# A two-layer encoder trunk in fp32: the layer norms' shift row as a TensorE product, and own buffers for the modulation vectors' products

## The chip, the cores and the metric

The kernel runs on one core of one Trainium2 chip. The metric is the device time of one execution in microseconds (us). A core has five engines with an instruction queue each: PE (TensorE, matrix products; its weight loads are shown as PEld), DVE (VectorE), ACT (ScalarE), POOL (GpSimd) and SP (SyncE, which here only issues DMAs). An engine executes its own queue in order and waits on semaphores for the others.

## The reference

One sequence of 512 tokens with 1024 features goes through two layers, each a token mixer and an MLP. The modulation vectors come from a small conditioning vector c.

```python
for i in range(2):                       # layer 0: windowed attention, layer 1: RG-LRU block
    shift, scale, gate = split(silu(c) @ ada_w[i, 0] + ada_b[i, 0], 3)
    y = mixer[i](x * (1 + scale) + shift)
    x = layer_norm(ALPHA * x + (1 + gate) * y, ln_g[i, 0], ln_b[i, 0])
    shift, scale, gate = split(silu(c) @ ada_w[i, 1] + ada_b[i, 1], 3)
    y = square(relu((x * (1 + scale) + shift) @ mlp_w1[i])) @ mlp_w2[i]
    x = layer_norm(ALPHA * x + (1 + gate) * y, ln_g[i, 1], ln_b[i, 1])
```

There are four layer norms. The first three are followed by a modulated input of the next sublayer; called norm 0 (after attention), norm 1 (after the first MLP) and norm 2 (after the recurrent block) here. All matrices are float32 and are read once from DRAM.

## The kernel before, in words

**Products.** A float32 matrix product is done as three products in the fp32r format: each operand is split into a rounded part `hi` and a remainder `lo`, and hi*hi, hi*lo and lo*hi are summed in PSUM (`mm3`). Weights arrive by DMA in units of 128x1024 (512 KB) in one of four buffers `raw`. `conv_unit` splits a unit into one of six buffers `w`: ACT writes the rounded part (a CAST in the profile), DVE subtracts to get the remainder (a TENSOR_TENSOR `w<-raw,w`). The weight stream is strictly in order over the whole kernel.

**Order.** Python calls first only record operations (`Program.add`). A planner (`schedule`) then plays them through with estimated costs (`price`) and priorities (the place in the program plus an offset that the code shifts by the numbers in the table `P`) and so fixes the order of each engine's queue; `emit` (line 483) issues them. So nearly every instruction in the profile has line L483, and is told apart by its tiles. The DMA queue of SP has a fixed order too: a DMA that waits for its buffer holds all behind it.

**Stages.** Attention first (the QKV products, then eight heads one after the other, then the output projection), norm 0, the first MLP, norm 1, the recurrent block with norm 2, the second MLP and the last norm. The tokens are in four blocks `t` of 128. A sublayer's last products (`out_tiles`) come block by block, and `last_sink` follows each with `evac` (adds the residual, takes row statistics) and `ln_block`.

**A norm block** (`ln_block`, line 819). For each half `fh` of 512 features ACT normalizes in place, then DVE does two operations, `u = xh * rows[3]` and `h = u + rows[4]` (lines 859 and 860; `ex<-xb,rows` and `ex<-ex,rows` in the profile), where `rows[3]` and `rows[4]` hold gain and shift of norm and modulation together, copied to all 128 partitions. PE transposes `h` in four 128x128 pieces into one PSUM bank, and the split of that bank into `ht` (ACT and DVE) is the input of the next sublayer. A DMA from POOL that accumulates adds `ALPHA * ln_b` to the residual (line 881). The next sublayer's first products are done for token blocks 0 and 1 first and then 2 and 3 (`m_tiles` with `nsplit`).

**The combined rows** (`mod_rows`, line 787): three DVE operations over 128x1024 and two of ACT.

**Modulation vectors** (`gemv_tasks`, line 731). A vector of 1024 needs eight weight pieces of 128x1024; each is loaded into a `raw` buffer, and DVE multiplies it by a column of silu(c) and adds it to an accumulator (SCALAR_TENSOR_TENSOR `rows<-raw,sc,rows` or `acc<-raw,sc,acc`). At the end the 128 partitions are summed, by PE (attention) or POOL (first MLP). There are three vectors in attention and seven in the first MLP. They are cut into tasks that are called between the heads (`BH` tasks after each) or weight units. `keep_raw = 2` leaves two of the four `raw` buffers to them.

Of the kernel before, what the change touches and what calls it, by code (L numbers as in the profile page):

```python
# [70 lines left out]
def pack(inp):  # L71
# [91 lines left out]
    out["ident"] = np.eye(128, dtype=np.float32)  # L163
    return out
# [13 lines left out]
class View:  # L178
# [55 lines left out]
class Program:  # L234
# [60 lines left out]
    def price(self, op, reads, writes):  # L295
# [40 lines left out]
    def schedule(self):  # L336
# [36 lines left out]
        while len(order) < total:  # L373
# [101 lines left out]
    def emit(self, nc, tc, pools):  # L475
        fix = lambda a: self.real(a, pools)
        with tc.manual_schedule():
            order = self.schedule()
            self.place(order, pools)
            for op in order:  # L480
                args = [fix(a) for a in op.args]
                kw = {k: fix(a) for k, a in op.kw.items()}
                op.ins = getattr(getattr(nc, op.eng), op.fn)(*args, **kw)  # L483
# [3 lines left out]
        [128, "ht", "rows", "acc2"]  # L487
        + [f"ex{i}" for i in range(17) if i not in (12, 13)]
# [5 lines left out]
        + [f"hid{i}" for i in range(16)]  # L494
# [36 lines left out]
class Kernel:  # L531
    def __init__(self, I, O):
# [6 lines left out]
        self.ht = t("ht", 8192)  # L539
        self.hid = [t(f"hid{i}", 512) for i in range(16)]  # L540
        self.xb = [t(f"xb{i}", 1024) for i in range(TB)]
        self.rx = t("rows", 6144)
        self.rows = [self.rx[:, 1024 * i : 1024 * i + 1024] for i in range(5)]
        self.ex = [t(f"ex{i}", 512) if i not in (12, 13) else self.rx[:, 512 * i - 1024 : 512 * i - 512] for i in range(17)]
        self.ident = t("ident", 128)
# [12 lines left out]


    def renew(self, kind, idx):  # L560
        n = {"hid": 512, "xb": 1024, "ex": 512, "w": 2048}[kind]
        for i in idx:
            getattr(self, kind)[i] = self.region(f"{kind}{i}", n)
# [87 lines left out]
    def HT(self, k, lo=0, hi=512):  # L651
        a = k * 512
        return self.ht[:, a + lo : a + hi].bitcast(F32R), self.ht[:, 4096 + a + lo : 4096 + a + hi].bitcast(F32R)
# [5 lines left out]
    def fill(self):  # L659
# [16 lines left out]
        BH=3,  # L676
        QE='aavavavava',
        PE='ava',
        BO=(-100, 0, 100),
# [5 lines left out]
        AP0='vvvvvvvv',  # L685
# [16 lines left out]
        XV=(1, 1, 1),  # L702
    )
# [27 lines left out]
    def gemv_tasks(self, idx, part, acc, dst, sink_row=None, red=None, ap="vvvvvvvv"):  # L731
# [4 lines left out]
        def load(k):  # L736
            def f():
                if k < KT:
                    assert self.free_r
                    r = self.free_r.pop(0)  # L740
                    state[k] = r
                    nc.sync.dma_start(
                        out=self.raw[r][:, :], in_=self.I["adaw"][idx, k * 128 : (k + 1) * 128, part * D : (part + 1) * D]
                    )
# [3 lines left out]
                if k > 0:  # L748
                    r = state.pop(k - 1)
                    raw, c = self.raw[r][:, :], self.sc[:, k - 1 : k]  # L750
                    how = ap[k - 1]
                    if how != "v":
# [7 lines left out]
                    self.free_r.append(r)  # L760
# [26 lines left out]
    def mod_rows(self, shift, tmp):  # L787

        v = self.nc.vector
        r = self.rows  # L790
        v.scalar_tensor_tensor(out=tmp, in0=r[3][:, :], scalar=1.0, in1=r[2][:, :], op0=ALU.add, op1=ALU.mult)
        v.tensor_tensor(out=r[4][:, :], in0=shift, in1=tmp, op=ALU.add)
        v.scalar_tensor_tensor(out=r[3][:, :], in0=r[3][:, :], scalar=1.0, in1=r[1][:, :], op0=ALU.add, op1=ALU.mult)
        for i in (1, 2):
            self.nc.scalar.activation(out=r[i][:, :], in_=r[i][:, :], func=AF.Copy, scale=ALPHA)
# [23 lines left out]
    def ln_block(self, t, last=False, parts=1):  # L819
# [18 lines left out]
        for fh in range(2):  # L838
# [28 lines left out]
            hv = self.ht[:, a : a + 2048].rearrange("p (k n) -> p k n", k=4)[:, :, t * 128 : t * 128 + 128]  # L867
            lv = self.ht[:, 4096 + a : 4096 + a + 2048].rearrange("p (k n) -> p k n", k=4)[:, :, t * 128 : t * 128 + 128]
# [93 lines left out]
    def setup(self):  # L962
# [12 lines left out]
        self.mods = [Tile_("dr", f"mods{i}", 1024) for i in range(4)]  # L975
# [41 lines left out]
    def attn(self):  # L1017
# [7 lines left out]
        def OT(h, lo=0, hi=512):  # L1025
# [3 lines left out]
            a = (i - 4) * 1024  # L1029
            return self.ht[:, a + lo : a + hi].bitcast(F32R), self.ht[:, a + 512 + lo : a + 512 + hi].bitcast(F32R)  # L1030
# [88 lines left out]
        self.renew("ex", range(10))  # L1119
        self.keep_raw = 2  # L1120
# [29 lines left out]
        for n in range(2):  # L1150
# [6 lines left out]
            late.append((p, Q(6 + n, 0, 512)))  # L1157
        self.rope(late, self.P["QE"][8:])
# [85 lines left out]
        for h in order:  # L1244
# [7 lines left out]
        self.renew("ex", range(10))  # L1252
        self.renew("hid", range(8, 16))
        self.flush_bg()
        self.modes = self.P["OM"]
        self.mod_rows(accv, r[4])
# [45 lines left out]
    def load_mods(self, gate, shift, scale, ln, tmp):  # L1302
# [35 lines left out]
    def rnn(self, nsplit):  # L1338
# [6 lines left out]
        self.renew("ex", range(3, 9))  # L1345
        self.renew("hid", range(14, 16))
        xr = [self.hid[14][:, :], self.hid[15][:, :], ex[16][:, :]]
        XC = [ex[j] for j in range(3)]
        XCH = [ex[3 + j] for j in range(3)]
        XCL = [ex[6 + j] for j in range(3)]  # L1350
        GEL = [ex[9 + j] for j in range(3)]
# [126 lines left out]
        self.load_mods(0, 1, 2, 2, self.acc2)  # L1478
# [3 lines left out]
        self.renew("ex", range(3, 9))  # L1482
# [6 lines left out]
    def build(self, stop=99):  # L1489
# [3 lines left out]
        if stop == 1:  # L1493
            return self.dump()
        accs, red = (self.acc2, self.rows[1][:, :]), self.ex[8:10]
        gemvs = [(1, 2, self.rows[0], None), (2, 1, self.rows[3], None), (2, 0, self.rows[4], None)]
# [4 lines left out]
        self.bgq.append(lambda: self.mod_rows(self.rows[4][:, :], self.acc2))  # L1501
        self.bgq.append(self.rnn_cols)
        self.keep_raw, self.bg_rate = 2, self.P["RATE"]
# [12 lines left out]
        self.load_mods(3, None, None, 3, self.acc2)  # L1516
# [33 lines left out]
```

## Time and profile before

| | |
|---|---|
| median of 3 runs | 1193.3 us (1191.2 to 1193.58) |
| profiled execution | 1195.24 us |
| its span, first to last instruction | 1193.3 us |
| PE busy | 1137.3 us, 95% |
| DVE busy | 838.3 us, 70% |
| ACT busy | 523.7 us, 44% |
| mean granted clock of PE | 0.983 |
| weights read, 184 + 80 pieces of 512 KB seen in the records | 42% of the DMA engines' time on SP's queue |

The difference between the profiled execution and its span is time ahead of the first and behind the last instruction. Matmuls overlap, so PE's busy time counts a standing PE only where nothing is in flight; in a window of time the number of PE instructions shows a slow stretch as well. A window's row gives its length, then for PE, PEld, DVE, ACT and POOL the busy time and the number of instructions, the granted clock (1.00 is full), the DMA engines' share and GB/s. A timeline's row gives start, length, engine, line, operation, tiles and the number of merged instructions, and in brackets how long the engine stood idle ahead of it and what ended that.

### The profile page before, as it was taken

Reading aid. Unit: us, or ns where it says so; the run is one execution under the profiler, and the core shown is the slowest. Engines: PE = TensorE matmul, PEld = TensorE weight load, DVE = VectorE, ACT = ScalarE, POOL = GpSimd, SP = SyncE. Lnnn points to the kernel's source line nnn. Section 1 sums busy time; section 2 is a strip of 40 time slices with the busy share of each in tenths; the row PEclk is TensorE's granted clock in tenths of the full one; section 3 lists DMA queues with packets and bytes.
Section 4 is the critical chain, followed back from the end, with each engine's and each line's share of the span. In section 5 each row is a group of like instructions: output and inputs, shape, how many; then the busy total and the mean of one; then the engine's idle time right before and its main releaser. Section 6 shows DMA issues by size and latency. Waiting matters only on the chain.

```text
span 1193.3 us, 14277 instructions
## 1 busy us (share of the span) xinstructions
PE 1137.3 (95%) x5268; PEld 929.6 (78%) x5268; DVE 838.3 (70%) x1253; ACT 523.7 (44%) x774; POOL 95.7 (8%) x66
## 2 busy tenths in 40 slices
PE   6989998999999999999999998979999999999995
PEld 4877667988788878887887876868888888888885
DVE  8876979878878975449848888699744444444447
ACT  5455645512321342324368989824522322322411
POOL 1000000122222220000000000000100000000004
PEclk9999998999999999999999998989999999999998
DMA  9752663767677654222534574543732222222201
GB/s 348 287 188 76 212 246 106 196 210 247 200 246 244 247 195 154 100 95 55 151 106 121 139 181 111 151 142 125 211 106 89 99 95 91 104 88 106 89 1 71
DMA packets 56683, 179.99 MB, mean 151 GB/s; under 512 B 7891, under 2 KB 8403, under 8 KB 56614
## 3 DMA queue, kind: packets, MB, share of 16 engines
q1 hardware_dynamic: 53590, 170.44, 42.1%
q0 software_dynamic: 3024, 8.65, 4.0%
q8 instruction: 41, 0.67, 0.2%
q14 instruction: 28, 0.23, 0.1%
HBM read 160.56 MB, written 2.11 MB: 136 GB/s over the span
## 4 chain that ended last, share of the span: by engine, by line
PE 60%; DVE 16%; DMA 8%; ACT 8%; issue 4%; POOL 2%; SPq 1%; DVEq 0%; ACTq 0%; POOLq 0%
PE ps L483 60%; DVE ex L483 4%; DVE w L483 3%; DMA raw<-in_adaw 3%; DVE rows L483 3%; ACT w L483 2%; ACT rows L483 2%; POOL ex L483 2%; DVE xb L483 2%; DVE acc L483 2%; DMA rows<-w 1%; ACT L483 1%; DMA rows<-rows 1%; DVE st L483 1%; ACT ex L483 1%
## 5 line engine op out<-in xcount | busy, mean ns | idle before, releaser
L483 PE MATMUL ps<-ht,w 128*128 128x512 f32 (+1 forms) x2664 | 557.7, 370 | 3.1 <-ACT ht L483 1.8
L483 PEld LDWEIGHTS ps<-ht,w 128*128 128x128 f32 x2664 | 461.4, 190 | 90.1 <-ACT ht L483 2.7
L483 PE MATMUL ps<-w,hid 128*128 128x512 f32 (+1 forms) x1800 | 414.3, 390 | 2.2 <-ACT w L483 1.4
L483 DVE TENSOR_TENSOR w<-raw,w 128x1024 fp32r<-128x1024 f32 x192 | 237.2, 1240 | 226.7 <-ACT w L483 226.4
L483 PEld LDWEIGHTS ps<-w,hid 128*128 128x128 f32 x1800 | 334.1, 188 | 75.6 <-ACT w L483 1.8
L483 ACT CAST w<-raw 128x1024 fp32r<-128x1024 f32 x192 | 198.4, 1040 | 409.6 <-PE ps L483 304.8
L483 PE MATMUL ps<-w,ht 128*128 128x512 f32 (+1 forms) x336 | 75.5, 376 | 6.3 <-DVE w L483 5.2
L483 PEld LDWEIGHTS ps<-w,ht 128*128 128x128 f32 x336 | 57.5, 193 | 19.3 <-DVE w L483 5.6
L483 DVE SCALAR_TENSOR_TENSOR acc<-raw,sc,acc 128x1024 f32<-128x1024 f32 x40 | 55.4, 1385 | 17.1 <-DMA raw<-in_adaw 17.0
L483 DVE SCALAR_TENSOR_TENSOR ex<-rows,ps 128x512 f32<-128x512 f32 (+1 forms) x81 | 53.0, 671 | 19.7 <-PE ps L483 19.7
L483 DVE SCALAR_TENSOR_TENSOR rows<-raw,sc,rows 128x1024 f32<-128x1024 f32 x40 | 55.7, 1394 | 14.3 <-DMA raw<-in_adaw 14.1
L483 ACT ACTIVATE rows<-ps 128x512 f32<-128x512 f32 x66 | 39.1, 593 | 55.8 <-PE ps L483 55.7
L483 DVE TENSOR_TENSOR xb<-xb,ex 128x512 f32<-128x512 f32 (+1 forms) x81 | 55.8, 701 | 1.1 <-ACT xb L483 0.5
L483 DVE TENSOR_TENSOR hid<-ex,hid 128x512 fp32r<-128x512 f32 x66 | 45.5, 690 | 6.4 <-ACT hid L483 1.3
L483 DVE TENSOR_TENSOR ex<-rows 128x512 f32<-128x512 f32 x64 | 47.4, 742 | 1.6 <-ACT rows L483 1.5
L483 ACT ACTIVATE hid<-rows 128x512 fp32r<-128x512 f32 x64 | 40.5, 633 | 1.9
L483 ACT ACT_TABLE_LOAD x26 | 33.4, 1283 | 3.2 <-DMA w<-w 2.0
L483 PE MATMUL ps<-ident,ex 128*128 128x128 f32 x124 | 21.7, 294 | 13.6 <-DVE ex L483 13.5
L483 POOL TENSOR_TENSOR ex<-xb,rows 128x512 f32<-128x512 f32 x5 | 6.8, 1378 | 328.7 <-ACT xb L483 328.7
L483 POOL DMA_DIRECT2D xb<-rows x12 | 11.0, 919 | 262.3 <-DVE mv L483 136.3
L483 DVE TENSOR_TENSOR rows<-rows,ex 128x512 f32<-128x512 f32 x32 | 20.6, 683 | 15.4 <-DMA rows<-rows 12.4
L483 ACT ACTIVATE xb<-xb,mv 128x512 f32<-128x512 f32 x29 | 22.3, 810 | 19.9 <-DVE mv L483 19.8
(142 smaller groups left out, 803.8 us busy)
## 6 DMA issues: line engine op xcount, KB each, us to landing
raw<-in_W SPq DMA_DIRECT2D x184, 512.0 KB
raw<-in_adaw SPq DMA_DIRECT2D x80, 512.0 KB
ex<-in_ada0t SPq DMA_DIRECT2D x28, 256.0 KB
xb<-rows POOLq DMA_DIRECT2D x12, 512.0 KB, 5.9
rows<-w SPq DMA_DIRECT2D x16, 192.0 KB
raw<-in_W SPq DMA_DIRECT2D x8, 288.0 KB
rows<-rows SPq DMA_DIRECT2D x36, 64.0 KB
xb<-in_xT SPq DMA_DIRECT2D x8, 256.0 KB
```

Source lines behind the costliest of these rows:

```text
L483: op.ins = getattr(getattr(nc, op.eng), op.fn)(*args, **kw)
```

## The change

1. **Shift row.** The second DVE operation of a half block (line 860) goes; `h` is written by the multiplication alone. The shift is added after the transposes by one more fp32r product into the same bank: its weights `bm` hold the shift of that half as 4 rows of 128 features (rounded part in rows 0 to 3, remainder in rows 32 to 35), its moving operand `sel` is a 36x512 matrix of ones and zeros that spreads row j over columns 128j to 128j+127. The four transposes and the product are one accumulation group: only the first transpose opens the bank.
2. **Combined rows.** `mod_rows` keeps one of its three 1024-wide DVE operations. Shift and scale are written to DRAM as rows and read back as 4x256, with the norm's bias as `lnb4`, and combined there by DVE, ACT and POOL operations of 4x256 and less. The 512 KB broadcast of the shift ahead of norm 2 goes.
3. **Own buffers.** The modulation pieces no longer use `raw`: in attention they have two 128x1024 buffers of their own, and from the fourth head on six (four of them in the half of `ht` that is then free); in the first MLP three. `keep_raw` is 0. For this, several `ex` and `hid` buffers become halves of 1024-wide pairs, `ht` becomes two tiles, and the recurrent block's buffers are renumbered. The scratch of the recurrent block's column constants (`ex[10]`) thereby lies in one of the modulation buffers.
4. **Order.** Five tasks after each head, not three; their priority in attention is no longer raised by 100. Four of the eight pieces of the attention gate are multiplied by ACT and added by an accumulating DMA from POOL. The planner's costs for POOL's DMAs are refined.

```diff
         elif op.eng == "gpsimd" and op.fn == "dma_start":
-            op.cost = 1000
+            op.nbytes = w.shape[0] * n * 4
+            op.cost = 870 if "accum_op" in op.kw else 500
...
                 if op.fn == "dma_start":
-                    op.end += 4000
+                    if "accum_op" in op.kw:
+                        op.end += 5000 if op.nbytes > 300000 else 2600
+                    else:
+                        op.end += 2700 if op.nbytes > 100000 else 1500
...
+                if op.fn == "transpose" and kw:
+                    op.ins = nc.tensor.matmul(args[0], lhsT=args[1], rhs=args[2], is_transpose=True, stop=False, skip_group_check=True, **kw)
+                    continue
...
+        self.ex[0], self.ex[2] = self.pair("exa")
+        self.ex[4], self.ex[6] = self.pair("exb")
+        self.ex[10:12] = self.pair("exc")
+        self.big = [a[:, :].tile[:, :] for a in (self.ex[10], self.hid[10], self.ex[0], self.ex[4])]
...
-        BH=3,
+        BH=5,
-        BO=(-100, 0, 100),
+        BO=(0, 0, 100),
-        AP0='vvvvvvvv',
+        AP0='avavavav',
+        OWN=(0, 2, 3),
+        SW=3,
...
-                    assert self.free_r
-                    r = self.free_r.pop(0)
-                    state[k] = r
+                    state[k] = self.own[self.n_big % len(self.own)]
+                    self.n_big += 1
...
-                        nc.gpsimd.tensor_tensor(out=acc, in0=raw, in1=acc, op=ALU.add)
+                        nc.gpsimd.dma_start(out=acc, in_=raw, accum_op=ALU.add)
...
-    def mod_rows(self, shift, tmp):
+    def mod_rows(self, ln, shift, scale):
-        v.scalar_tensor_tensor(out=tmp, in0=r[3][:, :], scalar=1.0, in1=r[2][:, :], op0=ALU.add, op1=ALU.mult)
-        v.tensor_tensor(out=r[4][:, :], in0=shift, in1=tmp, op=ALU.add)
         v.scalar_tensor_tensor(out=r[3][:, :], in0=r[3][:, :], scalar=1.0, in1=r[1][:, :], op0=ALU.add, op1=ALU.mult)
...
+        self.renew("ex", (8, 9))
+        sel, tmp = r[4][0:36, 0:512], [self.acc2[0:4, i * 256 : i * 256 + 256] for i in range(3)]
+        nc.sync.dma_start(out=sel, in_=self.I["sel"])
+        nc.scalar.copy(out=self.ex[9][0:36, :].bitcast(F32R), in_=sel)
+        nc.sync.dma_start(out=tmp[0], in_=self.I["lnb4"][ln])
+        for i, row in ((1, scale), (2, shift)):
+            nc.sync.dma_start(out=tmp[i].rearrange("p (f c) -> p f c", f=2), in_=self.mods[row][0:1, :].quarters())
+        v.scalar_tensor_tensor(out=tmp[1], in0=tmp[1], scalar=1.0, in1=tmp[0], op0=ALU.add, op1=ALU.mult)
+        v.tensor_tensor(out=tmp[2], in0=tmp[2], in1=tmp[1], op=ALU.add)
+        nc.gpsimd.memset(self.ex[8][0:36, 0:256], 0.0)
+        nc.scalar.copy(out=self.ex[8][0:4, 0:256].bitcast(F32R), in_=tmp[2])
+        v.tensor_tensor(out=self.ex[8][32:36, 0:256].bitcast(F32R), in0=tmp[2], in1=self.ex[8][0:4, 0:256], op=ALU.subtract)
...
-                (v if self.par("GE") == "v" else nc.gpsimd).tensor_tensor(out=u, in0=xh, in1=self.rows[3][:, c], op=ALU.mult)
-                v.tensor_tensor(out=h, in0=u, in1=self.rows[4][:, c], op=ALU.add)
+                v.tensor_tensor(out=h, in0=xh, in1=self.rows[3][:, c], op=ALU.mult)
...
-                nc.tensor.transpose(pt[:, j * 128 : j * 128 + 128], h[:, j * 128 : j * 128 + 128], self.ident[:, :])
+                nc.tensor.transpose(pt[:, j * 128 : j * 128 + 128], h[:, j * 128 : j * 128 + 128], self.ident[:, :], start=j == 0)
+            bm, sel = self.ex[8][0:36, fh * 128 : fh * 128 + 128].bitcast(F32R), self.ex[9][0:36, :].bitcast(F32R)
+            nc.tensor.matmul(pt[:, :], lhsT=bm, rhs=sel, start=False, stop=True, skip_group_check=True)
...
-        self.keep_raw = 2
+        self.keep_raw = 0
+        self.own = self.big[:2]
...
+        self.renew_ht()
+        own = self.region("htl", 4096)
+        more = self.own + [own[:, i * 1024 : i * 1024 + 1024] for i in range(4)]
...
+            if i == self.P["SW"]:
+                self.own = more
             head(h)
             self.bg(self.P["BH"])
...
-        self.mod_rows(accv, r[4])
+        for row, src in ((4, r[3]), (5, accv)):
+            nc.sync.dma_start(out=self.mods[row][0:1, :], in_=src[0:1, :])
+        self.mod_rows(0, 5, 4)
...
-            nc.sync.dma_start(out=self.rows[4][:, :], in_=self.mods[shift][0:1, :].partition_broadcast(128))
-            self.mod_rows(self.rows[4][:, :], tmp)
+            self.mod_rows(ln, shift, scale)
...
-        self.keep_raw, self.bg_rate = 2, self.P["RATE"]
+        self.own = [self.big[i] for i in self.P["OWN"]]
+        self.bg_rate = self.P["RATE"]
```

More of the change, by code (lines that the diff above doesn't have):

```diff
@@ L163, in pack @@
     out["ident"] = np.eye(128, dtype=np.float32)
+    out["lnb4"] = np.ascontiguousarray(out["lnb"].reshape(4, 2, 4, 128).transpose(0, 2, 1, 3).reshape(4, 4, 256))
+    sel = np.zeros((36, 512), np.float32)
+    for j in range(4):
+        sel[[j, 32 + j], j * 128 : j * 128 + 128] = 1.0
+    out["sel"] = sel
     return out
@@ L482, in emit @@
                 kw = {k: fix(a) for k, a in op.kw.items()}
+                if op.fn == "transpose" and kw:
+                    op.ins = nc.tensor.matmul(args[0], lhsT=args[1], rhs=args[2], is_transpose=True, stop=False, skip_group_check=True, **kw)
+                    continue
                 op.ins = getattr(getattr(nc, op.eng), op.fn)(*args, **kw)
     LAYOUT = (
-        [128, "ht", "rows", "acc2"]
-        + [f"ex{i}" for i in range(17) if i not in (12, 13)]
+        [128, "hth", "htl", "rows", "acc2", "exa", "exb", "exc"]
+        + [f"ex{i}" for i in (1, 3, 5, 7, 8, 9, 14, 15, 16)]
         + [f"raw{i}" for i in range(4)]
@@ L493 @@
         + [192]
-        + [f"hid{i}" for i in range(16)]
+        + [f"hid{i}" for i in range(10)]
+        + ["hida"]
+        + [f"hid{i}" for i in range(12, 16)]
     )
@@ L538, in __init__ @@
         self.raw = [t(f"raw{i}", 1024) for i in range(self.NR)]
-        self.ht = t("ht", 8192)
+        self.ht = [t("hth", 4096), t("htl", 4096)]
         self.hid = [t(f"hid{i}", 512) for i in range(16)]
+        self.hid[10:12] = self.pair("hida")
         self.xb = [t(f"xb{i}", 1024) for i in range(TB)]
@@ L557, in region, with pair @@
         return Tile_("sb", name, n)
+    def pair(self, name):
+        t = self.region(name, 1024)
+        return [t[:, 0:512], t[:, 512:1024]]
     def renew(self, kind, idx):
@@ L562, in renew, with renew_ht @@
         for i in idx:
-            getattr(self, kind)[i] = self.region(f"{kind}{i}", n)
+            if kind == "hid" and i in (10, 11):
+                self.hid[10:12] = self.pair("hida")
+            else:
+                getattr(self, kind)[i] = self.region(f"{kind}{i}", n)
+    def renew_ht(self):
+        self.ht = [self.region("hth", 4096), self.region("htl", 4096)]
     def small(self, tag, n=4):
@@ L738, in f @@
                 if k < KT:
-                    assert self.free_r
-                    r = self.free_r.pop(0)
-                    state[k] = r
-                    nc.sync.dma_start(
-                        out=self.raw[r][:, :], in_=self.I["adaw"][idx, k * 128 : (k + 1) * 128, part * D : (part + 1) * D]
-                    )
+                    state[k] = self.own[self.n_big % len(self.own)]
+                    self.n_big += 1
+                    nc.sync.dma_start(out=state[k], in_=self.I["adaw"][idx, k * 128 : (k + 1) * 128, part * D : (part + 1) * D])
                 if k == 0:
@@ L748, in f @@
                 if k > 0:
[L749 to L750 removed]
+                    raw, c = state.pop(k - 1), self.sc[:, k - 1 : k]
                     how = ap[k - 1]
@@ L974, in setup @@
         self.st = {}
-        self.mods = [Tile_("dr", f"mods{i}", 1024) for i in range(4)]
+        self.mods = [Tile_("dr", f"mods{i}", 1024) for i in range(6)]
         cT, sg = self.small("cT", 8), self.small("sg", 8)
@@ L1243, in attn @@
         uo = N_WQ + 4
-        for h in order:
+        for i, h in enumerate(order):
+            if i == self.P["SW"]:
+                self.own = more
             head(h)
@@ L1300, in mlp, with load_mods @@
                 self.out_tiles(b + 12, 4, self.HID, lambda t, p: self.evac(t, 1, p, False), 0)
-    def load_mods(self, gate, shift, scale, ln, tmp):
+    def load_mods(self, gate, shift, scale, ln):
         nc = self.nc
@@ L1343, in rnn @@
         NW = self.NW
-        self.renew("ex", range(3, 9))
+        self.renew("ex", (1, 3, 5, 7, 8, 9))
         self.renew("hid", range(14, 16))
         xr = [self.hid[14][:, :], self.hid[15][:, :], ex[16][:, :]]
[L1348 to L1351, printed above, removed]
+        XC = [ex[j] for j in (0, 2, 4)]
+        XCH = [ex[j] for j in (1, 3, 5)]
+        XCL = [ex[j] for j in (7, 8, 9)]
+        GEL = [ex[j] for j in (6, 10, 11)]
         RI = {(i, j): self.rx[:, n * 512 : n * 512 + 512] for i in range(4) for j in range(3) for n in ((j * 3 + i) if i < 3 else 9 + j,)}
@@ L1500, in build @@
         self.bgq.append(lambda: self.load_ln_rows(1))
-        self.bgq.append(lambda: self.mod_rows(self.rows[4][:, :], self.acc2))
+        self.bgq.append(lambda: self.mod_rows(1, 5, 4))
         self.bgq.append(self.rnn_cols)
-        self.keep_raw, self.bg_rate = 2, self.P["RATE"]
+        self.own = [self.big[i] for i in self.P["OWN"]]
+        self.bg_rate = self.P["RATE"]
         self.ln_index = 1
```

34 lines of the change are left out of this document (19 added, 15 removed).

## The prediction

> **What bounds the kernel now.** I read the page's busy times first, then the windows by stage, then the waits, and the timeline of each place where TensorE (PE) stands still.
>
> ```profile
> PE 1137.3 (95%) x5268; PEld 929.6 (78%) x5268; DVE 838.3 (70%) x1253; ACT 523.7 (44%) x774; POOL 95.7 (8%) x66
> ...
> 59.50:189.00 129.50, 121.56 (x557) 90.42 (x555) 101.71 (x212) 72.59 (x159) 1.91 (x2) 0.99 0.52 175
> 189.00:198.00 9.00, 3.38 (x18) 2.55 (x17) 9.00 (x21) 5.05 (x8) 0.00 (x0) 0.81 0.35 117
> 198.00:558.70 360.70, 358.38 (x1681) 297.94 (x1680) 273.94 (x339) 117.29 (x151) 60.13 (x25) 1.00 0.56 183
> 558.70:577.00 18.30, 13.52 (x95) 12.28 (x94) 17.40 (x35) 8.02 (x13) 1.71 (x2) 0.91 0.46 109
> 577.00:842.00 265.00, 250.81 (x1163) 205.83 (x1162) 214.58 (x315) 188.53 (x277) 11.15 (x13) 0.97 0.47 137
> ...
> 860.00:1140.00 280.00, 280.00 (x1224) 229.68 (x1224) 126.93 (x154) 84.00 (x105) 0.00 (x0) 1.00 0.27 95
> ```
>
> The columns of a window are its length, then PE, PEld, DVE, ACT, POOL busy, the granted clock, DMA share and GB/s. From 860 to 1140 us, in the second MLP, PE is busy throughout: 280 us / 1224 = 0.229 us for a 128x512 product. Nothing but fewer products would help there, and the change takes none away. PE's idle time sits elsewhere: attention 129.5 - 121.56 = 7.9 us, layer norm 0 (after attention) 9.0 - 3.38 = 5.6, first MLP 2.3, layer norm 1 (after that MLP) 18.3 - 13.52 = 4.8, and 14.2 in the recurrent stage. In the two layer-norm windows VectorE (DVE) is busy for 9.00 of 9.00 and 17.40 of 18.30 us, so there DVE sets the pace. The waits say the same:
>
> ```profile
> PE ps L483 <- DVE ex L483: 13.5, 7, 4.3
> ...
> SPq L483 <- DVE w L483: 608.8, 163, 23.1
> ```
>
> A row is total us, times, longest. PE's largest wait is for `ex`, the normalized block that DVE hands to the transposes. The second row is the DMA queue waiting for a `raw` buffer to come free.
>
> **The change part by part.** First the shift row. Each half block loses one DVE addition, and each norm loses two 1024-wide DVE operations of `mod_rows`:
>
> ```profile
> L483 DVE TENSOR_TENSOR ex<-ex,rows 128x512 f32<-128x512 f32 x24 | 15.6, 682 | 0.0
> L483 DVE TENSOR_TENSOR rows<-rows,acc 128x1024 f32<-128x1024 f32 x2 | 2.4, 1216 | 0.0
> L483 DVE SCALAR_TENSOR_TENSOR mv<-mv 128x1 f32<-128x1 f32 x31 | 6.2, 240 | 0.1
> L483 PE MATMUL ps<-ex,w 96*128 96x512 f32 x108 | 26.4, 400 | 0.7 <-ACT rows L483 0.7
> ...
> 189.73 1.28 DVE L483 TENSOR_TENSOR ex<-ex,rows 128x512 f32<-128x512 f32 x2
> 190.46 1.26 PE L483 MATMUL ps<-ident,ex 128*128 128x128 f32 x8 [1.27 <-DVE ex L483]
> ...
> 195.34 1.28 DVE L483 TENSOR_TENSOR ex<-ex,rows 128x512 f32<-128x512 f32 x2
> 196.07 1.97 PE L483 MATMUL ps<-ident,ex 128*128 128x128 f32 x8 [4.35 <-DVE ex L483]
> ...
> 197.86 4.96 PE L483 MATMUL ps<-ht,w 128*128 128x256 f32 x26
> ```
>
> The 24 additions start about 0.6 us apart (a pair takes 1.28), so a norm loses 8 x 0.6 = 4.8 us of DVE, and `mod_rows` 2 x 1.2 = 2.4. It gains three DVE operations of 4x256: between 0.24 us (the 128x1 row) and 0.68 (the 128x512 row), taken in the middle at 0.4, because half the width is nearest to neither; 1.2 us together. PE gains 24 products of 36x512. A 96-row one costs 26.4 / 108 = 0.24 against 0.23 at 128 rows, so rows do not matter: 24 x 0.23 = 5.5 us, which costs nothing only where PE would stand idle.
>
> Layer norm 0: MLP products start at 197.86, after block 1, and DVE has had no idle time since 189. Ahead of that lie 4 additions and the two `mod_rows` operations, 2.4 + 2.4 - 1.2 = 3.6 us. The gate, scale and shift products also leave: four of DVE's steps now sit between 162 and 173 us, just ahead of the norm:
>
> ```profile
> 162.39 1.28 DVE L483 SCALAR_TENSOR_TENSOR rows<-raw,sc,rows 128x1024 f32<-128x1024 f32 x1
> ...
> 171.76 1.27 DVE L483 SCALAR_TENSOR_TENSOR rows<-raw,sc,rows 128x1024 f32<-128x1024 f32 x1
> ```
>
> With 5 tasks a head in place of 3 they come earlier. That is worth between 0 and 3.8 us more, since 5.6 us idle and 1.8 us of slow products (26 in 4.96 us is 0.19 each; at the 0.123 of the norm-2 row below they would take 3.2) bound the place at 7.4. I take 5.5, the middle. The trace shows the clock at 0.81 here. The Trainium skill ("TensorE: Matmul & The Clock Gate", "What's actually happening") says that PE falls to half rate after an idle window of about 3.4 us; with 4.35 us cut by 3.6 that window never fills, and by the rule alone the time would be some 1.8 us lower.
>
> Layer norms 1 and 2:
>
> ```profile
> 575.15 1.28 DVE L483 TENSOR_TENSOR ex<-ex,rows 128x512 f32<-128x512 f32 x2
> 575.88 0.66 PE L483 MATMUL ps<-ident,ex 128*128 128x128 f32 x4 [2.31 <-DVE ex L483]
> ...
> 833.58 5.67 PE L483 MATMUL ps<-ht,w 128*128 128x256 f32 x46
> ...
> 840.35 1.28 DVE L483 TENSOR_TENSOR ex<-ex,rows 128x512 f32<-128x512 f32 x2
> 841.09 1.32 PE L483 MATMUL ps<-ident,ex 128*128 128x128 f32 x8 [1.84 <-DVE ex L483]
> ...
> 842.42 12.81 PE L483 MATMUL ps<-ht,w 128*128 128x256 f32 x104
> ```
>
> In norm 1 the last block releases PE at 575.88; all 8 additions lie ahead of it in DVE's order, 4.8 us, less 0.3 for the product that the evacuation now waits for: 4.5 (ends 2.4, if only the 4 additions of blocks 2 and 3 count, and 4.8). In norm 2 PE's products end at 833.58 + 5.67 = 839.25 and go on at 842.42; of these 3.2 us, 0.9 are the transposes: 2.3 gained (ends 0.5, 2.3). There PE is the bound after that.
>
> End of the recurrent stage:
>
> ```profile
> 788.83 1.22 DVE L483 SCALAR_TENSOR_TENSOR acc<-rows 128x1024 f32<-128x1024 f32 x1
> ...
> 790.56 1.22 DVE L483 TENSOR_TENSOR rows<-rows,acc 128x1024 f32<-128x1024 f32 x1
> ...
> 792.84 1.22 DVE L483 TENSOR_TENSOR w<-raw,w 128x1024 fp32r<-128x1024 f32 x1
> ...
> 794.11 19.66 PE L483 MATMUL ps<-w,ht 128*128 128x512 f32 x74 [5.21 <-DVE w L483]
> ```
>
> PE waits 5.21 us for the weight remainder at 792.84, and two operations that go, 2 x 1.14 us by their spacing, stand ahead of it. The small ones that replace them may stand there too or later: 1.6 (ends 0, 2.3).
>
> Products with own buffers, first MLP: weights get all four `raw` buffers and the modulation three of their own.
>
> ```profile
> 325.96 0.74 PE L483 MATMUL ps<-w,hid 128*128 128x512 f32 x2 [1.37 <-ACT w L483]
> ...
> 442.41 7.83 PE L483 MATMUL ps<-w,hid 128*128 128x512 f32 x33 [0.86 <-DVE w L483]
> ```
>
> These two stalls are nearly all of its 2.3 us. The first waits for a cast of a weight, which an earlier load permits earlier; the second stands behind `mod_rows`. 1.9 gained (ends 0, 2.3).
>
> Attention: the same buffers, later priority for the tasks, and four of the gate's eight pieces go by ACT and an accumulating DMA from POOL.
>
> ```profile
> 78.69 4.53 PE L483 MATMUL ps<-hid,ex 128*128 128x256 f32 x10 [3.85 <-DMA ex<-rows]
> ...
> 151.66 1.28 DVE L483 SCALAR_TENSOR_TENSOR rows<-raw,sc,rows 128x1024 f32<-128x1024 f32 x1 [2.94 <-DMA raw<-in_adaw]
> ...
> 153.68 0.44 PE L483 MATMUL ps<-ident,ex 128*128 128x128 f32 x2 [1.86 <-DVE ex L483]
> ...
> DMA to landing us min/median/max: 4.4/5.9/8.4
> ```
>
> At 151.66 a modulation step waits 2.94 us for its load, softmax work is queued behind it on DVE, and PE loses 1.86. That goes. The 3.85 at 78.69 is the rotary embedding's DMA and mostly stays; a modulation step of 1.28 us ahead of it may move. I take 3.0 (ends -10 and 7.9): the last row is the landing of the existing accumulating DMAs; where one lands at the longest and not the median, 2.5 us later, DVE's next step waits with the softmax behind it, four times, 10 us. I take the gain, since the median is what the new cost table assumes (0.87 + 5.0). DVE loses 4 x 1.28 = 5.1 us, ACT gains about as much at 44% busy, POOL four issues at 8%.
>
> Moved and free: per norm SP issues four small DMAs more (selector, bias, two quarters; norms 0 and 1 also write shift and scale to DRAM), 0.33 us each by the second row below, and norm 2 one 512 KB broadcast less. Write, read, three DVE operations and a copy are about 2.2 + 2.2 + 2 = 6.4 us, by the 2.2 us of a small DMA here:
>
> ```profile
> 66.64 2.18 DMA ex<-rows
> ...
> 775.02 0.33 SPq L483 DMA_DIRECT2D rows<-mods  x1
> ...
> 176.38 0.59 ACT L483 COPY acc<-ps 128x512 f32<-128x512 f32 x1
> ...
> 218.65 0.26 DVE L483 TENSOR_SCALAR s<-ex 128x24 f32<-128x24 f32 x2
> ```
>
> In norm 0 the shift is ready at 177 (third row) and the first block at 190: hidden by the output projection's products; without that cover each us late costs one. The last row ends the recurrence's column constants, 33 tiny operations now at 214 to 219; their scratch becomes half of a modulation buffer, so they move behind the last product, near 435, under PE-bound work, and are due by 577. The new layout, the pairs and the single bank opening add no instruction.
>
> Sum: 3.0 + 5.5 + 1.9 + 4.5 + 1.6 + 2.3 = 18.8 us gained; of the 24 new products some 4 fall into idle time, 20 x 0.23 = 4.6 us paid: 14.2 us net. The profiled execution took 1195.24 (span 1193.3), so 1181.0; the median of the runs, 1193.3, is 1.9 lower: 1179.
>
> **The rivals.** *Larger gain*: norm 0 and attention give all they have (7.4 and 6), 4.9 more: 1174, and lower with the other ends; all ends together are 7.9 + 7.4 + 2.3 + 4.8 + 2.3 + 2.3 - 1.8 = 25.2, so 1168. For it: DVE's full windows. Against: DVE stays the one that is full there, 9.00 us in 9.00.
> *Small gain*: the stall passes to the row statistics, the ACT passes or the weight remainders that lie between, so that DVE's saving is only half PE's: 9.4 - 4.6 = 4.8 us, 1188.5. For it: between 190.46 and 196.07 DVE also did weight and `ht` remainders.
> *No change*: the shift row costs as much on PE as it frees and the buffers were not what was waited for: 1193.
> *Slower*: the accumulating DMAs in attention. Each delays a step on the in-order DVE, and the modulation load behind it holds SP, where weights queue. The attention gain of 3 is then lost, 11.2 us stay, and it decides from 11.2 / 4 = 2.8 us beyond the assumed 5.9, that is from 8.7 us of landing, against a longest of 8.4 now; at 11 us the four cost 20: 1193.3 - 11.2 + 20 = 1202. The Trainium skill ("SBUF — State Buffer", "SBUF: two separate sides") says that DVE operations of a two-port mode keep POOL from writing such a DMA's descriptors, which it measured as 3.1 us in place of 0.62; as an estimate from that page, 4 x 2.5 = 10 us, and the time would be 1192. The spread from 4.4 to 8.4 agrees with a delay of that size.
>
> **How the numbers follow.** Forecast, 1173 to 1187: 0.55. Larger gain, below 1173: 0.12. Small gain, 1187 to 1191: 0.13. No change within 0.2% (2.4 us, about what a measurement here can tell): 0.08. Slower: 0.12. Faster is 0.55 + 0.12 + 0.13 = 0.80. A range of 1168 to 1192 leaves out the slower case, a part of no change and the tail of the larger gain, about 0.2.
>
> **What would show it.** In the profile after: no `ex<-ex,rows` additions, 24 new products, DVE some 20 us less busy; in norm 0 the wait of 4.35 us below 1.5, the one at 575.88 about gone, none at 839; 794.11's wait near 3.5; the second MLP unchanged to 1 us. The forecast is wrong if PE's waits in attention grow (DVE behind a DMA into `rows`), if PE waits for the shift operand before a first block, or if the new plan opens waits where none are now.

## The result, and the profile after

| | before | after |
|---|---|---|
| median of the runs | 1193.4 us (1191.2 to 1194.9, 6 runs) | 1184.9 us (1184.8 to 1189.3, 6 runs) |
| profiled execution | 1195.24 us, span 1193.3 | 1187.53 us, span 1185.7 |

The ratio of the changed kernel to the one before is 0.994, with a 95% interval of 0.9921 to 0.9958; a second set of executions gave 0.9919 (0.9902 to 0.9935). So the change makes the kernel faster, by 8.5 us in the first set and 9.4 in the second. The direction was forecast, and 1184.9 lies in the range; but 14.2 us were forecast.

The page's busy times and the same windows as before:

```profile
PE 1146.8 (97%) x5292; PEld 932.8 (79%) x5292; DVE 822.9 (69%) x1228; ACT 530.3 (45%) x784; POOL 100.6 (8%) x73
...
59.50:189.00 129.50, 121.78 (x554) 90.43 (x553) 99.34 (x212) 77.50 (x166) 6.51 (x7) 0.97 0.61 194
189.00:198.00 9.00, 9.00 (x43) 7.00 (x42) 6.99 (x18) 6.61 (x9) 0.00 (x0) 0.90 0.59 167
198.00:558.70 360.70, 360.19 (x1687) 297.78 (x1687) 276.12 (x334) 119.99 (x156) 60.44 (x26) 1.00 0.52 179
558.70:577.00 18.30, 16.64 (x111) 14.50 (x110) 13.87 (x30) 6.92 (x11) 1.71 (x2) 0.91 0.63 161
577.00:842.00 265.00, 257.89 (x1218) 210.49 (x1217) 212.00 (x311) 193.39 (x284) 11.47 (x14) 0.99 0.49 139
860.00:1140.00 280.00, 280.00 (x1225) 229.66 (x1224) 125.14 (x151) 82.41 (x103) 0.00 (x0) 1.00 0.26 91
```

Two things are to be seen. First, the stalls went nearly as the prediction said: norm 0's window was 3.38 us busy of 9.00 and is now full, and PE's idle time from 577 to 842 fell from 14.2 us to 7.1. (The faster kernel does somewhat other work in a window of the same times; a comparison at equal work stands below.) Second, PE itself is busy 9.5 us longer (1137.3 to 1146.8), where 24 products at 0.23 us should have added 5.5. The idle time fell by 17.1 us (1193.3 - 1137.3 to 1185.7 - 1146.8); over half of that came back as busy time. The timeline of one block in the first MLP, where PE is the bound, shows how (PE first, then the weight loads):

```profile
545.45 0.60 PE L500 MATMUL ps<-ident,exa 128*128 128x128 f32 x4
545.98 0.49 PE L502 MATMUL ps<-ex,ex 36*128 36x512 f32 x1
546.40 0.66 PE L500 MATMUL ps<-ident,exa 128*128 128x128 f32 x4
546.99 0.50 PE L502 MATMUL ps<-ex,ex 36*128 36x512 f32 x1
547.41 1.88 PE L502 MATMUL ps<-w,hid 128*128 128x512 f32 x7
...
545.22 0.59 PEld L500 LDWEIGHTS ps<-ident,exa 128*128 128x128 f32 x4
545.98 0.18 PEld L502 LDWEIGHTS ps<-ex,ex 36*128 36x128 f32 x1 [0.17 <-issue]
546.39 0.42 PEld L500 LDWEIGHTS ps<-ident,exa 128*128 128x128 f32 x4 [0.24 <-DVE xb L502]
...
547.41 1.45 PEld L502 LDWEIGHTS ps<-w,hid 128*128 128x128 f32 x7 [0.25 <-issue]
```

Four transposes and the product take 0.95 us (545.45 to 546.40) and 1.01 (546.40 to 547.41). In the kernel before, eight transposes took 0.79, so four take 0.40, and the product costs about 0.58:

```profile
549.66 1.04 PE L483 MATMUL ps<-ident,ex 128*128 128x128 f32 x8
550.45 1.86 PE L483 MATMUL ps<-w,hid 128*128 128x512 f32 x7
```

The weight loads say why. A load usually starts while the product before it still runs (the transposes' first load at 545.22, they themselves at 545.45). That of the 36-row product starts with its product, 0.17 us after the last load ended, and the load behind it waits 0.24 us (the name DVE there is only the last semaphore: behind the second product the same 0.25 us stand with nothing waited for). So no weight load is taken ahead at either boundary; I read it as PE emptying before and after each of these products. The theory for the experiments is thus that the price of the product, 0.23 us, was the wrong term, and that its row count sets it. The rival is that adding onto a bank that transposes have just written is what costs. A second question was what had become of attention, which, counted up to the transposes at 194.46, seemed to take 134.9 us in place of 129.5.

### The profile page after: what moved, and what is told of

Its sections match the earlier page's. It is cut to its first block, busy times and chain, and to the rows that moved or that the text cites. A ratio compares the mean times of both kernels' runs of the same rounds, so it can differ in the third digit from the quotient of the medians.

```text
span 1185.7 us, 14389 instructions
## 1 busy us (share of the span) xinstructions
PE 1146.8 (97%) x5292; PEld 932.8 (79%) x5292; DVE 822.9 (69%) x1228; ACT 530.3 (45%) x784; POOL 100.6 (8%) x73
## 4 chain that ended last, share of the span: by engine, by line
PE 70%; DVE 11%; ACT 8%; DMA 7%; issue 3%; SPq 0%; DVEq 0%; ACTq 0%
PE ps L502 69%; DVE w L502 3%; ACT rows L502 3%; DVE rows L502 2%; ACT w L502 2%; ACT L502 1%; DMA rows<-rows 1%; DMA raw<-in_W 1%; DVE ex L502 1%; PE ps L500 1%; DVE acc L502 1%; DVE xb L502 1%; DMA rows<-w 1%; ACT ex L502 1%; ACT acc L502 1%
## 5 line engine op out<-in xcount | busy, mean ns | idle before, releaser
L502 PE MATMUL ps<-hth,w 128*128 128x512 f32 (+1 forms) x1776 | 505.4, 369 | 2.8 <-ACT hth L502 1.8
L502 PEld LDWEIGHTS ps<-hth,w 128*128 128x128 f32 x1776 | 321.8, 190 | 61.8 <-ACT hth L502 1.9
L502 PE MATMUL ps<-w,hid 128*128 128x512 f32 (+1 forms) x1581 | 368.9, 390 | 0.0
L502 PEld LDWEIGHTS ps<-w,hid 128*128 128x128 f32 x1581 | 295.1, 189 | 64.4 <-issue 0.7
L502 PE MATMUL ps<-htl,w 128*128 128x512 f32 (+1 forms) x888 | 326.8, 368 | 0.0
L502 PEld LDWEIGHTS ps<-htl,w 128*128 128x128 f32 x888 | 168.1, 189 | 29.4 <-issue 0.7
L502 PE MATMUL ps<-w,hth 128*128 128x512 f32 (+1 forms) x256 | 68.4, 373 | 2.8 <-DVE w L502 1.7
L502 DVE SCALAR_TENSOR_TENSOR ex<-rows,ps 128x512 f32<-128x512 f32 (+1 forms) x81 | 53.2, 674 | 13.8 <-PE ps L502 13.7
L502 PEld LDWEIGHTS ps<-w,hth 128*128 128x128 f32 x256 | 45.3, 188 | 13.0 <-DVE w L502 2.1
L502 PE MATMUL ps<-w,hida 128*128 128x512 f32 (+1 forms) x219 | 54.2, 388 | 0.0
L502 PEld LDWEIGHTS ps<-w,hida 128*128 128x128 f32 x219 | 40.9, 188 | 8.8
```

## The experiments

All ratios are to the kernel before, executed on the same chip in the same set; medians in us.

**128 rows.** Zero rows are added to both operands of the shift product:

```
-    sel = np.zeros((36, 512), np.float32)
+    sel = np.zeros((128, 512), np.float32)
...
-    nc.gpsimd.memset(self.ex[8][0:36, 0:256], 0.0)
+    nc.gpsimd.memset(self.ex[8][0:128, 0:256], 0.0)
```

> The shift row's product gets 128 rows in place of 36 (the added rows of both operands are zeros), nothing else changes. Theory A, the 36-row product is dear because its weight load isn't taken ahead of it: the 24 products go from a pace of 0.42 us or more to about 0.23, the weight loads' idle time of 4.0 us ahead of them goes, and of 24 x 0.2 to 0.3 us some 20 in 24 are on the path, so 4 to 6 us less than the changed kernel: 1179 to 1181 us, a ratio to before of 0.988 to 0.990. Rival B, it is dear because it adds onto a bank that the transposes have just written: rows change nothing, 1185 us, ratio 0.993, and the idle time of 4.0 us stays.

Measured: 1178.3 against 1196.4, ratio 0.9848 (0.9829 to 0.9867); theory A holds, with a gain larger than its 4 to 6 us. PE's busy time is 1133.0 us, 13.8 below the changed kernel's. The groups of PE and its weight loads, then one block of this kernel:

```profile
L502 PE MATMUL ps<-ex,ex 128*128 128x512 f32 x24 | 11.5, 478 | 0.0
L502 PEld LDWEIGHTS ps<-ex,ex 128*128 128x128 f32 x24 | 4.6, 190 | 0.0
...
540.04 0.60 PE L500 MATMUL ps<-ident,exa 128*128 128x128 f32 x4
540.40 0.48 PE L502 MATMUL ps<-ex,ex 128*128 128x512 f32 x1
540.71 0.60 PE L500 MATMUL ps<-ident,exa 128*128 128x128 f32 x4
541.07 0.48 PE L502 MATMUL ps<-ex,ex 128*128 128x512 f32 x1
541.39 0.85 PE L502 MATMUL ps<-w,hid 128*128 128x512 f32 x3
```

Three and a half times the rows, the same columns, and the unit takes 0.67 us where it took 0.95 and 1.01: 0.28 for the product. Note that the group's mean duration hardly differs (478 ns to 496); the starts tell, not the durations. The rival with the bank falls.

**64 rows and 68 rows**, by the same edit.

> The shift row's product gets 64 rows in place of 36 (zeros again). Theory, what counts is that the product leaves rows of the array unused in halves (up to 64 rows): as with 36, idle time of about 4 us ahead of the 24 weight loads, a pace of 0.42, the changed kernel's time within 2 us. Rival, the cost falls with every row added: about 0.33, and 3 us less than the changed kernel. Rival, what counts is that 36 isn't a multiple of 32: no idle time, and the time of the 128-row kernel, 0.985 of before.

> The same with 68 rows. Theory: just over half of the rows is as good as all of them: no idle time ahead of the weight loads, a pace of 0.23 to 0.25, and 6 to 8 us less than the changed kernel, ratio 0.985 to 0.988. Rival, the cost falls with every row: 0.33, 3 us less. Rival, multiples of 32: as the changed kernel.

Measured, beside the changed kernel once more in the same set:

> The changed kernel once more, beside the three below on one chip, so that small differences can be read. Expected: 7 to 9 us less than before (ratio 0.992 to 0.995); the granted clock between 84 and 100 us, 0.86 in the profile shown, near 1.00 if it was a matter of that one execution, and then the first MLP starts some 2 us earlier.

| kernel | median | ratio | 95% interval |
|---|---|---|---|
| changed kernel (36 rows) | 1186.1 | 0.9919 | 0.9902 to 0.9935 |
| 64 rows | 1187.5 | 0.9933 | 0.9916 to 0.9951 |
| 68 rows | 1179.1 | 0.9878 | 0.9858 to 0.9899 |
| before | 1195.5 | | |

The groups of the weight loads with 36 rows (changed kernel), 64 and 68; the last column is the idle time before them:

```profile
L502 PEld LDWEIGHTS ps<-ex,ex 36*128 36x128 f32 x24 | 4.4, 183 | 4.0 <-issue 4.0
```

```profile
L502 PEld LDWEIGHTS ps<-ex,ex 64*128 64x128 f32 x24 | 4.4, 183 | 4.0 <-issue 4.0
```

```profile
L502 PEld LDWEIGHTS ps<-ex,ex 68*128 68x128 f32 x24 | 4.8, 200 | 0.0
```

The starts say the same: four transposes and the product take 0.96 us with 64 rows (543.45 to 544.41) and 0.67 with 68 (536.54 to 537.21). 64 rows pay in full, 68 pay nothing: a step between the two, neither a slope nor a matter of multiples of 32. The Trainium skill ("TensorEngine Tiling (Array Packing)", "Key Properties") says that changing the tiling mode, not just the tile, drains the TensorE. The Trainium skill (the same page, "When to Use Tiling") gives row tiling for contract dimensions up to 64. The step between 64 and 68 and the 4.0 us of idle time agree with both; that a product of 36 or 64 rows switches this mode is my reading, no run shows the mode itself. The Trainium skill gives no price; here it is about 0.3 us for each change there and back. The clock between 84 and 100 us was 0.88 in this execution too, so that part of the expectation for the repeated kernel is wrong: it wasn't a matter of one execution.

**Two products in place of one.** Behind each shift product a second one with zero weights, onto the same bank, with 36 rows and with 128:

```
     nc.tensor.matmul(pt[:, :], lhsT=bm, rhs=sel, start=False, stop=False, ...)
+    nc.tensor.matmul(pt[:, :], lhsT=zero, rhs=sel, start=False, stop=True, ...)
```

> The changed kernel, and behind each 36-row product a second one of 36 rows whose weights are zeros, onto the same bank (24 more). If the price is paid where the row count changes (full array to half and back), the second product costs its columns alone, about 0.23 us: 24 x 0.23 = 5.5 us more than the changed kernel, 1190 to 1193, and idle time of about 4 us ahead of the weight loads as before. If each small product pays by itself, the second costs 0.4 to 0.6 as well: 10 to 14 us more, 1195 to 1200, and twice the idle time.

> The same with 128 rows in both: 24 more full products. Expected 24 x 0.23 = 5.5 us, less what falls beside waits, more than the 128-row kernel: 1182 to 1185, 0.988 to 0.991 of before. It gives what a full product costs on the path, and what the 36-row product's extra cost is to be compared with.

Measured against 1195.4: with 36 rows 1192.6, ratio 0.9971 (0.9956 to 0.9987), and with 128 rows 1186.1, ratio 0.9920 (0.9893 to 0.9948). One block with 36 rows twice, and its weight loads:

```profile
547.28 0.60 PE L500 MATMUL ps<-ident,exa 128*128 128x128 f32 x4
547.81 0.73 PE L502 MATMUL ps<-ex,ex 36*128 36x512 f32 x2
548.47 0.66 PE L500 MATMUL ps<-ident,exa 128*128 128x128 f32 x4
...
L502 PEld LDWEIGHTS ps<-ex,ex 36*128 36x128 f32 x48 | 7.3, 190 | 4.2 <-issue 4.2
```

The unit grew from 0.95 us to 1.19: the second small product costs 0.24, and the idle time stays at 4.2 though there are twice as many. So the price is that of the change of row count, not of a small product. The 128-row pair came out 1 us above its expectation; in its profile PE waits 2.89 us for a block of norm 0 where the single product's waits 0.42, and I didn't follow that further. The 36-row pair waits 2.0 us there, the changed kernel 0.3. So the pairs' whole times hold such a wait beside the products, and the price is better read from the block above.

**The parts alone.** The buffers without the shift product, and the shift product without the buffers:

```
# buffers alone: the changed kernel with
+    v.tensor_tensor(out=h, in0=u, in1=self.rows[4][:, c], op=ALU.add)
-    nc.tensor.matmul(pt[:, :], lhsT=bm, rhs=sel, ...)
-    self.mod_rows(0, 5, 4)
+    self.mod_rows(accv, r[4])
# shift product alone: the kernel before, with these lines the other way round
```

> The modulation's own buffers, its task rates and the accumulating DMAs in attention stay, the shift row is added by DVE again (old layer norm and old row preparation). Theory, attention's loss comes with the buffers and the norms' gain with the product: attention takes about 134 us, the norms stall as before, first MLP without its two stalls: 1193.4 + 5 - 2 = 1196, between 1193 and 1199. Rival, the buffers give what was forecast for them (3 in attention, part of norm 0, 1.9 in the first MLP): 1186 to 1189.

> The kernel before with the shift row's product and the new row preparation alone; old buffers, old task rates, gate vector by DVE. Theory, the norms gain by the product what the first expectation's products leave: norm 0 some 3.6, norm 1 4.5, recurrent stage 1.6 to 3.5, norm 2 2.3 to 5, together 12 to 16, less 20 x 0.45 = 9 for the products: 3 to 7 gained, 1186 to 1190, attention unchanged at 129.5. Rival, attention's loss comes with the shift row: attention takes 134 us here too, and the time is 1191 to 1195.

Measured: buffers alone 1199.1, ratio 1.0029 (1.0013 to 1.0046); shift product alone 1193.7, ratio 0.9982 (0.9969 to 0.9995). Alone, the buffers cost 2.7 us and the product gains 2.8; together they give 8 to 9. To see where, I compared executions at equal work: for the start of each PE instruction, how many columns had been streamed by then, the new products left out (2,408,452 in each kernel), and so the difference in time to the kernel before, taken at the ends of its stages. Minus is time gained in the stage, in us, each from one profiled execution:

| stage (us in the kernel before) | after | after, again | 68 rows | 128 rows | buffers alone | product alone |
|---|---|---|---|---|---|---|
| 0 to 60, set-up | +1.5 | +1.1 | +0.5 | +1.5 | +1.1 | +0.5 |
| 60 to 180, attention | -0.8 | -2.4 | -5.9 | -2.4 | -4.0 | +0.1 |
| 180 to 220, norm 0 | -0.9 | -2.1 | -3.7 | -4.7 | -8.2 | -3.5 |
| 220 to 540, first MLP | -2.8 | -2.9 | -2.8 | -2.9 | +9.8 | +1.6 |
| 540 to 600, norm 1 | -1.1 | +0.4 | -3.5 | -4.8 | +0.9 | +0.3 |
| 600 to 780, recurrent | -0.2 | +0.4 | +1.0 | +1.0 | +2.1 | +0.4 |
| 780 to 800, its end | -5.6 | -5.4 | -6.1 | -5.6 | +0.2 | -5.2 |
| 800 to 860, norm 2 | +1.7 | +1.7 | +0.3 | +0.3 | +4.9 | +1.7 |

(Attention differs by some us between executions: -5.9 is one in which PE's wait for the rotary embedding was 1.3 us and not 3.4 to 4.6. The executions shown for 68 rows, 1175.3 us, and for the buffers alone, 1202.1, lie 4 us below and 3 above their medians; the table shows where time goes rather than how much. Part of such differences is the clock, as the next section shows.) The theory that attention had lost by the buffers falls: it gained in each kernel with them. So the buffers alone came to the upper end of the forecast 1193 to 1199 by luck, and the product alone came into its rival's range without the rival's cause, since its attention is unchanged (+0.1). Attention's window looked longer because parts of the output projection, whose products run between norm 0's blocks, had moved. And buffers alone empty norm 0's stall by 8.2 us, more than with the product, and then lose 9.8 in the first MLP: PE waits there for weight remainders, between 200 and 400 us (total, times, longest):

```profile
PE ps L502 <- DVE w L502: 7.4, 3, 3.8
```

In the changed kernel the longest such wait there is 0.3 us.

**Norm 0 by DVE, norms 1 and 2 by a 128-row product**, to see whether norm 0 needs the product at all:

```
+    if self.ln_index == 0:
+        v.tensor_tensor(out=u, in0=xh, in1=self.rows[3][:, c], op=ALU.mult)
+        v.tensor_tensor(out=h, in0=u, in1=self.rows[4][:, c], op=ALU.add)
```

> The kernel with 128-row products, but layer norm 0 adds its shift row on DVE again; norms 1 and 2 by the product. Theory, norm 0's stall went with the modulation steps that were moved ahead of it and not with the shift row (buffers alone started the first MLP at 187.89 us, the 128-row product at 192.35): the first MLP starts 3 to 4 us earlier than with the product and the time is 1174 to 1176, 0.982 of before. Rival, the DVE time that comes back there is missed in the first MLP, as with the buffers alone, where PE waited 7.4 us more for weight remainders: the time is that of the 128-row kernel or up to 5 us more.

Measured: 1183.8, ratio 0.9902 (0.9889 to 0.9915). By the ratios that is some 6 us more than the 128-row kernel, and 4.8 more than the 68-row kernel of the same set; the rival holds, at the upper end of its 5 us or just past it. At equal work norm 0 gains 8.3 us, 3.6 more than in the 128-row kernel, but the first MLP loses 4.6 where that one gains 2.9. This wait of PE is there, with what DVE and POOL do at that time:

```profile
243.76 14.54 PE L502 MATMUL ps<-w,hid 128*128 128x512 f32 x56 [6.66 <-DVE w L502]
...
231.40 8.01 POOL L502 PARTITION_ALL_REDUCE rows<-acc  x2 [21.29 <-DVE acc L502]
...
234.06 2.18 DVE L502 SCALAR_TENSOR_TENSOR rows<-exc,sc,rows 128x1024 f32<-128x1024 f32 x1 [1.00 <-DMA exc<-in_adaw]
236.16 2.80 DVE L502 TENSOR_TENSOR hida<-ex,hida 128x512 fp32r<-128x512 f32 x1
...
241.29 1.27 DVE L502 SCALAR_TENSOR_TENSOR rows<-exa,sc,rows 128x1024 f32<-128x1024 f32 x1
242.49 1.21 DVE L502 TENSOR_TENSOR w<-raw,w 128x1024 fp32r<-128x1024 f32 x1
```

So DVE time that norm 0's additions take, 4.8 us, is missed 50 us later, in the first MLP's weight remainders. That it is missed there is shown by these two kernels: the sum over partitions behind the same modulation steps starts at 231.40 here and at 227.75 in the 128-row kernel, 3.7 us later. The wait has other parts too: beside that sum two operations take 2.18 and 2.80 us in place of 1.28 and 0.68, and DVE waits 1.00 us for a load; the 128-row kernel has such slow operations as well, earlier, and PE does not wait for them. How I read it is that own buffers let the modulation steps come in a denser row on DVE, and that only the shift row's DVE time makes room for them, so that the parts don't add up. That reading is not shown: each kernel is planned anew, and another order of the queues may account for a part.

**The gate's pieces by DVE again** (`AP0='vvvvvvvv'`), to price the accumulating DMAs:

> In attention all eight pieces of the gate vector are added by DVE again, as before the change (no ACT scaling, no accumulating DMAs from POOL there); the rest is the changed kernel. Theory, the accumulating DMAs delay the rotary embedding's small DMAs and DVE's steps: the wait of 3.57 us ahead of 82.93 goes, attention takes 130 us or less from 59.5 in place of 134.9, and the time is 4 to 5 us less, 1180 to 1181. Rival, attention lost by something else of the change (more loads in flight, five tasks a head in place of three, the order of the rotary embedding): attention stays at 134 or more, and the time at 1185, or 1186 to 1189 where DVE's 4 x 1.28 us more count.

Measured: 1185.6, ratio 0.9911 (0.9889 to 0.9933), not to be told from the changed kernel's 0.9919. The windows from 72 to 84 and 84 to 100 us, of the changed kernel and of this one:

```profile
72.00:84.00 12.00, 7.68 (x30) 5.27 (x29) 6.95 (x16) 7.49 (x16) 0.87 (x1) 0.90 0.91 274
84.00:100.00 16.00, 15.76 (x62) 11.20 (x60) 11.12 (x36) 10.28 (x28) 0.85 (x1) 0.86 0.42 111
```

```profile
72.00:84.00 12.00, 10.71 (x42) 7.42 (x41) 11.24 (x25) 5.98 (x16) 0.00 (x0) 1.00 0.85 289
84.00:100.00 16.00, 11.96 (x48) 6.73 (x47) 14.62 (x31) 10.05 (x25) 0.00 (x0) 1.00 0.68 219
```

PE's wait for the rotary embedding does go from the first window, and comes back in the second in small waits behind a DVE that is busy 14.62 of 16 us. The theory was wrong that anything is gained by it. (The execution shown is the fastest of the six, 1180.1 us, with a mean granted clock of 0.995 where the changed kernel's has 0.988; the others took 1182.6 to 1189.1.)

The 128-row kernel is faster than this one and than the changed kernel; it can't be told from the one with 68 rows.

## Why the prediction was right and wrong

*The price of the 24 products (wrong, and the main miss).* The step was "A 96-row one costs 26.4 / 108 = 0.24 against 0.23 at 128 rows, so rows do not matter". The row came from the wrong side of a step: 96 rows are on the full array's side, 36 are not. 24 products at 0.58 us are 13.9 us in place of 5.5. On the chip the difference between 36 rows and full rows is 8.7 us (18.1 gained by 128 rows, 9.4 by the changed kernel in its second set) or 7.0 (16.4 by 68 rows, in the same set); the starts in the blocks give 24 x 0.30 = 7.2 of it. With full rows, at nearly the price forecast, the change gives 16 to 18 us, near the 14.2. That this is so near is in part luck: the end of the recurrent stage gave 4 us more than its term, norm 2 and attention less than theirs.

*End of the recurrent stage (size).* 1.6 forecast, 5.6 and 5.4 measured in the changed kernel, 5.2 with the product alone, nothing with the buffers alone. The wait at 794.11 was to be near 3.5 and is 1.71. The rest, about 2 us, is the clock. Windows of the kernel before and of the changed one, and the products behind the wait in each:

```profile
780.00:800.00 20.00, 14.53 (x52) 10.98 (x52) 17.34 (x22) 6.50 (x7) 0.00 (x0) 0.83 0.44 148
...
794.11 2.50 PE L483 MATMUL ps<-w,ht 128*128 128x512 f32 x5 [5.21 <-DVE w L483]
```

```profile
777.00:792.00 15.00, 12.97 (x55) 9.88 (x54) 14.90 (x20) 7.64 (x9) 0.00 (x0) 1.00 0.43 146
...
786.31 0.50 PE L502 MATMUL ps<-w,hth 128*128 128x512 f32 x1 [1.71 <-DVE w L502]
```

Before, 5.21 us of idle time were followed by ten products that start 0.43 us apart, half the pace of the 0.23 behind them; after 1.71 us there is no slow stretch. The prediction reckoned with the clock in norm 0 and forgot it here.

*Norm 0 (right on the stall, wrong on what follows).* 5.5 us were forecast, 0.9 and 2.1 measured, 4.7 with 128 rows. The wait of 4.35 us was to fall below 1.5. It is gone, products of the output projection now stand in its place; the one wait of size left, 1.17 us, is that ahead of the first block, 1.27 before. But eight products at 0.58 us are paid here, and in this execution the clock still fell:

```profile
185.00 0.63 PE L500 MATMUL ps<-ident,exa 128*128 128x128 f32 x4 [1.17 <-DVE exa L502]
...
184.30:187.70 3.40, 2.70 (x13) 1.78 (x14) 3.11 (x5) 1.90 (x4) 0.30 (x1) 0.96 0.00 0
187.70:191.20 3.50, 3.50 (x10) 2.77 (x9) 2.96 (x9) 0.72 (x1) 0.55 (x1) 0.55 0.76 150
...
187.68 3.69 PE L502 MATMUL ps<-w,hid 128*128 128x512 f32 x9
```

In the first stretch PE runs eight transposes, two shift products and three others beside the end of the wait, in the second it is full and has 0.55 of its clock, some 1.6 us lost. In the second execution the clock stays at 1.00 from 180 to 196. So the step "that window never fills" failed in one execution of two. The Trainium skill ("TensorE: Matmul & The Clock Gate", "Part 4: PE-mode transpose") adds that transposes don't count as PE-busy in the same way; these two rows agree with that. The Trainium skill (the same page, "What's actually happening") says that the window of about 3.4 us runs freely; that fits the two executions. In all traces here, after the first 20 us and ahead of the last 20, the clock stands at half for 3.4 or 6.8 us at a time.

*Norm 1 (wrong).* 4.5 us gained, less the products, was forecast; 1.1 us gained and 0.4 lost came, and 4.8 gained with 128 rows. The wait at 575.88 was to be about gone. With 36 rows (first two lines) and with 128 (last two) it is:

```profile
571.15 0.63 PE L500 MATMUL ps<-ident,exb 128*128 128x128 f32 x4 [1.66 <-DVE exb L502]
573.10:576.00 2.90, 2.90 (x11) 2.57 (x11) 1.16 (x2) 0.59 (x1) 0.86 (x1) 0.50 0.45 89
...
564.05 0.63 PE L500 MATMUL ps<-ident,exb 128*128 128x128 f32 x4 [1.87 <-DVE exb L502]
560.00:580.00 20.00, 18.13 (x127) 16.49 (x126) 16.21 (x30) 8.90 (x14) 1.71 (x2) 1.00 0.56 143
```

So full rows don't shorten the wait, and that their 4.8 us lie near the forecast is luck. What differs is the products' price, 8 x 0.30 = 2.4 us, and the clock behind the wait, 0.50 with 36 rows (in both executions) and 1.00 with 128. One execution with 128 rows doesn't show that full rows keep the clock up: with 68 rows it was at half for 3.4 us near this norm.

*First MLP (right).* 1.9 forecast, 2.8 and 2.9 measured: of both stalls 0.3 us is left, and the second MLP is unchanged at 280.00. *Norm 2 (right on the wait, the products mis-priced).* None is left at 839, but the products cost more than that gives: 2.3 less 1.8 was forecast, 1.7 were lost, with full rows 0.3.

*Attention (right in sign, not in its reasons).* 3.0 forecast, 0.8 and 2.4 measured, and 1.1 to 1.5 us lost in the set-up, which the prediction did not look at. The accumulating DMAs land in about the time assumed, 5.9 us (the last number is the median to landing; the four take 4.4 to 5.9):

```profile
rows<-exc POOLq DMA_DIRECT2D x4, 512.0 KB, 5.1
```

The slower rival needed 8.7, and the delay of POOL's descriptors that the prediction estimated from the Trainium skill doesn't show. But the 5.1 us that DVE saves there are worth nothing that can be measured: the kernel that gives them back takes the same time.

*The rival "small gain"* (1187 to 1191) came near the total but not the cause: the stalls did not pass to DVE's other work, TensorE's own time grew. *DVE some 20 us less busy* was 15.4. *The column constants* are 24 tiny operations of DVE, not 33; they moved to 405 to 418 us and no wait of PE stands there.

## What to carry to other kernels

A product with 36 or 64 rows among full ones was not a small product but two changes of row count: padding with zeros to 68 or 128 rows took the price away and cost nothing that shows. Read starts and the weight loads' idle time, since durations don't show it. Take a price from a row of the same kind only if it lies on the same side of such a step. And when work is taken from an engine, follow it past the stage it leaves: the DVE time of norm 0 paid in the first MLP, and neither half of the change paid alone.

## What the runs showed of the hardware

- A change from products of 128 rows to one of 36 and back costs TensorE about 0.3 us (0.58 against 0.28 us for the product); 64 rows cost the same (0.96 us with four transposes, against 0.67 for 68 rows and for 128); and two small products in a row pay once (0.24 for the second).
- The clock can fall to half without a long wait: 0.55 over 3.5 us after 1.17 us of idle time among transposes, 0.50 over 2.9 us after 1.66; and it can stay at 1.00 after 1.87. It stands at half for 3.4 or 6.8 us at a time (half rate from 194.7 to 201.5 us before, from 187.4 to 190.8 after), and each 3.4 us of it costs a busy PE 1.7; two executions of one kernel can differ by such a stretch.
- DVE slows beside POOL's all-reduce over partitions, in the changed kernel by more than twice: an operation that takes 1.28 us elsewhere takes 3.26.

```profile
231.41 6.81 POOL L502 PARTITION_ALL_REDUCE rows<-acc  x2 [16.00 <-DVE acc L502]
...
231.80 3.26 DVE L502 SCALAR_TENSOR_TENSOR rows<-exb,sc,rows 128x1024 f32<-128x1024 f32 x1
```
